# A decode step with paged attention: score and value products of four cached pages ranked ahead as one group

## The chip, the cores and the metric

The kernel runs on one core of a Trainium2 chip. The metric is the device time of one execution in microseconds (us); it is given as the median of three runs. Everything below that is read from a profile comes from one profiled execution on that core.

## What is computed

One inference step of a hybrid decoder layer, for a prompt of 512 tokens and a sample of 8 sequences with 4 new tokens each:

```python
z = rms_norm(x, g_mix) @ w_in              # columns: RWKV-7 | FoX | Conformer conv
ya = rwkv7_mix(za, ...); yb = fox_fn(q, k, v, logf); yc = conv_module(zc, ...)
x = x + concatenate([ya, yb, yc]) @ w_out
x = x + cross_attend(x, mk, mv, ...)       # 4 heads, 256 memory tokens
x = x + conv_ffn(x, ...)
```

The change touches one part of it, the sample's FoX attention over its cached keys and values (8 heads of 64 channels, 2048 cached tokens in 16 pages of 128 for each sequence; `kp` and `vp` are the pages that a table names):

```python
s_past = einsum('bqhd,bkhd->bhqk', q, kp) * scale + cT[..., :, None] + exT[..., None, :]
p = softmax(concatenate([s_past, s_new], axis=-1), axis=-1)
o = einsum('bhqk,bkhd->bqhd', p[..., :P], vp) + einsum('bhqk,bkhd->bqhd', p[..., P:], v)
```

All is float32. The large products with weights split both sides into a high and a low float32r part and add three products.

## The kernel before

One long function, `hybrid_step`, writes instructions through helpers (all matmuls stand on L186, all transposes on TensorE on L216). A scheduler then orders them: among the instructions that are ready for an engine it takes the one with the best rank, and the rank is the place in which the code wrote it, unless `tc.high_priority(n)` moves it ahead by n places. What comes out is a fixed order for each engine; each engine then goes through its own list, waiting where data or a buffer isn't there.

The stages follow each other: input norm and the first projection; RWKV, FoX and conv columns; the mixer's attention with the output projection; cross attention; feed-forward. The stage of this case is the mixer's attention. Two streams are woven in it (`weave`): `sample_past()`, the sample's attention over its cached pages, and `rest()`, which holds the end of the recurrence, the prompt's attention (`attend`, banks bank_r), the norm, keys and values of the memory (`memory`, products into bank_g from tiles xT, which first hold its operand), and the output projection `out_prompt` (products into bank_g from tiles four). The weave alternates their steps by estimated costs.

`sample_past` goes through the 8 batches. In round b it weaves `past_scores(b)` and `past_values(b - 2)`, with `past_weights(b - 1)` between. A step of either handles four of a batch's 16 pages, so that there are 32 steps of each:

- `past_scores`: POOL gathers four pages of keys into one of two buffers w_raw (`four_pages`, L1389: an indirect DMA, 128 partitions of 2048 numbers). DVE transposes them by blocks of 32 into one of two buffers KT (L1404). Then 16 products add into bank_s: four parts x of the channels by four strips of 32 rows (`QUAD`). Their stationary operand is 32 columns of Qx, which lies in a tile named w_hi. Behind the fourth step one product more (bank_s<-NX) adds the decay, the softmax's chain follows (L1299, L1415 to L1426), and bank_s is free for the next batch.
- `past_weights`: four transposes into bank_k and 16 small copies (L1439) make the weights PT, in a tile named w_lo.
- `past_values`: POOL gathers four pages of values into one of three buffers page (L1389). Then 4 products, one for each strip of 32 rows, add into bank_v; at the batch's end come four products with the step's own values (bank_v<-vs).

```python
            for x in range(4):
                for hp, po in enumerate(QUAD):
                    mm(acc[po, pg * 128: (pg + 1) * 128], Qx[:, 4 * hp + x]..., KT[:, :, 4 * hp + x], ...)
            yield 2.9
```

`sample_past` runs within `urgent(..., 0)`, which moves its instructions ahead by 0 places: they rank by where the weave puts them. In `out_prompt` POOL also adds squares (tot, L1670), each behind ACT (L1669).

Of the kernel before, what the change touches and what calls it, by code (L numbers as in the profile page):

```python
# [8 lines left out]
F32 = mybir.dt.float32  # L9
# [34 lines left out]
def _consts():  # L44
    """What depends on shapes alone: identities, masks, selections."""
# [46 lines left out]
    # rows (head, page of four, query) against pages, queries and columns of the like  # L92
# [18 lines left out]
def _past_consts():  # L111
    """of rows (head, page of four, query): causal mask, selections of pages, queries and columns"""
# [14 lines left out]
def _cross_consts():  # L127
    """of rows (head of two, 64 of the keys, token) those of a head and the 64; then selections of 32 rows, four times over"""
    p, m = np.arange(128)[:, None], np.arange(8)[None, :]
    own = [(m // 4 == h) & (m % 4 == p // 32) for h in range(2)]  # L130
    four = [p == 32 * x + np.arange(128)[None, :] % 32 for x in range(4)]
    return np.concatenate(own + four, 1).astype(np.float32)
# [5 lines left out]
def _pack_vectors(x):  # L138
    """Per-channel vectors side by side, a column for each 128 channels."""
# [15 lines left out]
def hybrid_step(tc, A):  # L155
# [62 lines left out]
    def rsqrt_from(out, in_, scale, eps):  # L218
        """out = (in * scale + eps) ** -0.5 by the logarithm and the exponential"""
        act(out=out, in_=in_, func=AF.Ln, scale=scale, bias=eps)  # L220
        act(out=out, in_=out, func=AF.Exp, scale=-0.5)

    def half_xyy(t, y, x, scale, eps):
        """t = (x * scale + eps) / 2 * y ** 2 for y, about the inverse root: (1.5 - t) * y is that root to the last bits"""
# [3 lines left out]
    def rsqrt_rows(out, x, n, scale, eps, eps_ap, work):  # L228
        """out = (x * scale + eps) ** -0.5 for n numbers to a partition"""
# [6 lines left out]
    def neg_sigmoid(t, e):  # L236
        """-1 / (1 + exp(-t)) in place, for t >= -40; by a Newton step"""
# [6 lines left out]
    def split(h, l, src, tt=vtt):  # L244
        """src = h + l exactly, both float32r"""
        acopy(h, src)
        tt(out=l, in0=src, in1=h.bitcast(F32), op=SUB)  # L247

# [18 lines left out]
    def weights(src, kb, cols, width=128, raws=None):  # L267
        """loads blocks of columns, two at most, and returns how to split each"""
# [37 lines left out]
    def gemm_steps(src, cols, xh, xl, evac, bank, spans=EVEN, kb=8, ahead=0, raws=None, first=None):  # L306
        """evac(ps, i, a) for span a of the i-th block of 128 columns; yields what each step costs TensorE"""
# [22 lines left out]
    def woven(*streams, first=False):  # L330
        """several streams side by side, each (its steps, their cost in all, where it sets in), in proportion; to the end of
        all or of the first"""
# [17 lines left out]
    def urgent(steps, ahead):  # L350
        """the steps, each before that many instructions of the others"""
# [27 lines left out]
    # what outlives the phases  # L379
# [16 lines left out]
    def four_blocks(n, dtype=F32R):  # L396
        """the places of four blocks of an operand, high or low"""
        return (yfp, yrp, xkp, xvp)[n].tile([128, 4, NT], dtype, name="four")

    yF = four_blocks(0, F32)  # first holds FoX's queries  # L400
# [5 lines left out]
    cum = cpl.tile([128, SEQ], F32R, name="cum")  # high parts from 0 and 64, low ones from 32 and 96  # L406
# [10 lines left out]
    # ================= inputs, first norm =================  # L417
# [20 lines left out]
    def norm_tok(xt, n, gain, ss, h, l, lo, work, bank, junk):  # L438
        """rows of xt, normed, transposed and split into columns lo.. of h and l"""
# [11 lines left out]
    # the operand is not yet divided by its root mean square: that follows after the products  # L451
# [4 lines left out]
    def roots(lo, n):  # L456
        """1 / root mean square of tokens lo .. lo + n, on all partitions"""
# [43 lines left out]
    # ================= gates of the cached keys =================  # L501
    # one row for each (batch, page), then (batch, head) by key, cumulated from the end
# [28 lines left out]
    # ================= RWKV columns, shifted by a token as they come =================  # L531
# [48 lines left out]
    # ================= RWKV: gates, keys, as their columns come =================  # L580
# [4 lines left out]
    def rmm(lhsT, rhs, evac):  # L585
        """float32 product with all 544 tokens of rhs, by halves"""
# [17 lines left out]
    def gates():  # L604
        """yields how many blocks of columns the next step needs"""
        yield 2
        # tanh(t) = 2 / (1 + exp(-2 t)) - 1
# [6 lines left out]
        # t1: minus the sigmoid of w, t4: that of a  # L614
# [6 lines left out]
        # decays: cumulated in each chunk, centred on half of the chunk's total  # L621
# [7 lines left out]
        # the step to the next chunk's centre, where that chunk's state will lie: [other half, block, head]  # L629
# [11 lines left out]
        # unit keys  # L641
# [40 lines left out]
    # where the cached keys and values lie: of four pages each, partition (page, k) takes rows 4 k .. 4 k + 3  # L682
# [13 lines left out]
    # ================= FoX and conv columns =================  # L696
# [9 lines left out]
    def finish(n=1):  # L706
        """what was put off until n more evacuations"""
# [5 lines left out]
    def evac_fl(ps, i, a):  # L713
        """forget gate: log_sigmoid(y) = -(max(-y, 0) + ln(1 + exp(-|y|)))"""
# [35 lines left out]
    def tok_major(dst, dst_s, src, src_s):  # L750
        """[128 channels, tokens] -> the prompt's token rows and the sample's"""
# [88 lines left out]
    def conv_taps():  # L840
        """the prompt's convolution: some taps on VectorE, the others by ScalarE and GpSimd"""
# [18 lines left out]
    def conv_ahead():  # L860
# [22 lines left out]
        for m in range(2):  # L883
            # the sample's windows, all taps at once: [batch * token, tap], by half the batches
# [11 lines left out]
    def rwkv_recurrence():  # L896
        def group_norm(y, n, heads, ps, work):
            """ps [n, heads, 64] -> y, each row of 64 centred and scaled"""
# [17 lines left out]
        # ================= RWKV: inverses of the blocks of 16 on the diagonals =================  # L916
        # N of (head, block of 128 tokens) as [chunk of two, block of 16, row] by column; with DVE's transposes by blocks
        # of 32 each of the 128 triangles comes to a partition (chunk, half, block of two, head and block of tokens)
# [48 lines left out]
        # ================= RWKV: sample, rows (head, batch, token) =================  # L967
        def sample_steps(rk, rk2):
# [43 lines left out]
            # -alpha S0 and rho S0, each row with its own batch  # L1012
# [37 lines left out]
            # the state after the four tokens  # L1050
# [18 lines left out]
        # ================= RWKV: chunks of 64, two to a block of 128 tokens =================  # L1069
# [4 lines left out]
        def chain(i, j, out):  # L1074
            """what a block and two heads need that no state enters, step by step"""
# [23 lines left out]
            # inverse of I - N by doubling blocks, from those of 16  # L1099
# [43 lines left out]
        def four(t, i):  # L1143
            """a block's columns as [head of two, its block, 64]"""
            return t[:, :, i * 128: (i + 1) * 128].rearrange("p j (r t) -> p j r t", r=2)

        def stateless(i):
            """of a block, in the places of what entered: AT (beta), RP (kap), the outputs (ynT) and the state (values) but for
            what the state before adds"""
# [36 lines left out]
        def stateful(i):  # L1186
            """the state, chunk after chunk: that of chunk ch lies in half ch % 2"""
# [51 lines left out]
    # what of the recurrence is left then runs beside the sample's attention  # L1239
# [38 lines left out]
    def recurrence_end():  # L1278
        """RWKV's group: ((norm * g + b) + bonus) * gate"""
# [9 lines left out]
        # where the residual will lie, the memory's operand  # L1289
# [3 lines left out]
        # causal mask, after nothing for the keys before  # L1293
# [7 lines left out]
    # ================= FoX: the prompt's attention, two heads at a time =================  # L1301
# [895 lines left out]
```

## Time and profile before

| | |
|---|---|
| median of three runs | 1304.64 us (1300.55 to 1308.29) |
| span of the profiled execution, first to last instruction | 1301.6 us; its own time isn't listed apart |
| TensorE (PE) busy | 1234.1 us, 95% |
| VectorE (DVE) busy | 809.1 us, 62% |
| ScalarE (ACT) busy | 501.2 us, 39% |
| GpSimd (POOL) busy | 290.6 us, 22% |
| moved by DMA | 173.83 MB, mean 134 GB/s |
| of it by POOL's queue, the gathers among it | 84.80 MB |

PE counts matmuls, PEld the loading of stationary operands, which runs beside them. Matmuls are pipelined, so that the records of matmuls that follow each other overlap: what a matmul adds is read from the chain of waits, where each piece begins at the end of the one before. "issue" is time in which an engine waited for nothing that the profile shows. A float32 product leaves two records in the trace.

### The profile page before, as it was taken

Reading aid. Unit: us, or ns where it says so; the run is one execution under the profiler, and the core shown is the slowest. Engines: PE = TensorE matmul, PEld = TensorE weight load, DVE = VectorE, ACT = ScalarE, POOL = GpSimd, SP = SyncE. Lnnn points to the kernel's source line nnn. Section 1 sums busy time; section 2 is a strip of 40 time slices with the busy share of each in tenths; the row PEclk is TensorE's granted clock in tenths of the full one; section 3 lists DMA queues with packets and bytes.
Section 4 is the critical chain, followed back from the end, with each engine's and each line's share of the span. In section 5 each row is a group of like instructions: output and inputs, shape, how many; then the busy total and the mean of one; then the engine's idle time right before and its main releaser. Section 6 shows DMA issues by size and latency. Waiting matters only on the chain.

```text
span 1301.6 us, 24852 instructions
## 1 busy us (share of the span) xinstructions
PE 1234.1 (95%) x10410; PEld 1011.6 (78%) x10410; DVE 809.1 (62%) x1514; ACT 501.2 (39%) x996; POOL 290.6 (22%) x322
## 2 busy tenths in 40 slices
PE   7899899999899999999998988999999999999997
PEld 6788788875555467654447875799999999999996
DVE  4699998765777377453234677557767424777631
ACT  5454543341456435221242422335444323444321
POOL 1262430033342131112223242012111100111120
PEclk9999999997699999999998998999999999999999
DMA  7221220221788497576663465033322323222231
GB/s 227 59 65 51 50 75 19 67 87 44 268 304 304 155 306 244 198 231 226 218 215 118 151 232 174 23 103 98 98 93 60 93 73 127 68 96 88 76 111 48
DMA packets 129649, 173.83 MB, mean 134 GB/s; under 512 B 7029, under 2 KB 110981, under 8 KB 121336
## 3 DMA queue, kind: packets, MB, share of 16 engines
q0 software_dynamic: 15216, 84.80, 18.1%
q1 hardware_dynamic: 88160, 70.76, 17.9%
q10 hardware_dynamic: 26160, 16.66, 4.4%
q8 instruction: 82, 1.34, 0.4%
q14 instruction: 31, 0.25, 0.1%
HBM read 164.54 MB, written 7.88 MB: 132 GB/s over the span
## 4 chain that ended last, share of the span: by engine, by line
PE 77%; DVE 9%; issue 5%; ACT 4%; DMA 3%; POOL 2%; SPq 0%; POOLq 0%; ACTq 0%; DVEq 0%
PE bank_g L186 42%; PE bank_r L186 10%; PE bank_d L186 6%; PE bank_s L186 6%; PE bank_v L186 4%; PE bank_a L186 2%; PE bank_r L216 2%; DVE w_lo L247 1%; PE bank_t L216 1%; PE bank_x L216 1%; DMA w_raw<-in_w_in_dram 1%; DMA w_raw<-in_w_out_dram 1%; DVE four L855 1%; DVE KT L1404 1%; ACT w_hi L177 1%
## 5 line engine op out<-in xcount | busy, mean ns | idle before, releaser
L186 PE MATMUL bank_g<-four,w_hi 128*128 128x272 f32 (+1 forms) x1536 | 284.7, 301 | 2.7 <-ACT w_hi L177 2.0
L177 ACT CAST w_hi<-w_raw 128x1024 fp32r<-128x1024 f32 (+3 forms) x149 | 140.6, 946 | 269.8 <-PE bank_g L186 206.1
L186 PEld LDWEIGHTS bank_g<-four,w_hi 128*128 128x128 f32 x1536 | 222.1, 189 | 26.4 <-issue 19.9
L247 DVE TENSOR_TENSOR w_lo<-w_raw,w_hi 128x1024 fp32r<-128x1024 f32 (+3 forms) x149 | 164.0, 1103 | 87.2 <-ACT w_hi L177 78.2
L186 PE MATMUL bank_g<-four,w_lo 128*128 128x272 f32 (+1 forms) x768 | 173.4, 301 | 0.5 <-DVE w_lo L247 0.5
L186 PEld LDWEIGHTS bank_g<-four,w_lo 128*128 128x128 f32 x768 | 122.1, 189 | 11.3 <-issue 8.6
L186 PE MATMUL bank_g<-act_h,w_hi 128*128 128x272 f32 (+2 forms) x400 | 124.6, 312 | 6.2 <-ACT w_hi L177 2.8
L186 PE MATMUL bank_g<-act_h,w_lo 128*128 128x272 f32 (+2 forms) x400 | 122.9, 308 | 0.0
L186 PE MATMUL bank_g<-act_l,w_hi 128*128 128x272 f32 (+2 forms) x400 | 122.0, 305 | 0.0
L2108 POOL TENSOR_SCALAR ysm<-HS,vec 128x32 f32<-128x32 f32 x44 | 42.0, 954 | 255.1 <-ACT HS L177 255.1
L1404 DVE STREAM_TRANSPOSE KT<-w_raw 128x2048 f32<-128x2048 f32 x32 | 73.5, 2302 | 23.9 <-PE bank_s L186 22.8
L186 PEld LDWEIGHTS bank_g<-act_h,w_hi 128*128 128x128 f32 x400 | 79.5, 199 | 10.5 <-ACT w_hi L177 3.2
L186 PEld LDWEIGHTS bank_g<-act_h,w_lo 128*128 128x128 f32 x400 | 79.1, 198 | 2.8 <-issue 1.2
L186 PEld LDWEIGHTS bank_g<-act_l,w_hi 128*128 128x128 f32 x400 | 79.4, 198 | 2.3 <-issue 1.1
L186 PE MATMUL bank_s<-KT,w_hi 128*32 128x128 f32 x1024 | 76.6, 292 | 3.4 <-DVE rsq L226 1.7
L186 PE MATMUL bank_d<-four,w_hi 128*128 128x272 f32 x384 | 78.1, 299 | 0.0
L186 PE MATMUL bank_g<-in_h,w_hi 128*128 128x272 f32 x352 | 73.6, 290 | 0.0
L186 PE MATMUL bank_g<-in_l,w_hi 128*128 128x272 f32 x352 | 73.5, 290 | 0.0
L186 PE MATMUL bank_g<-in_h,w_lo 128*128 128x272 f32 x352 | 73.2, 289 | 0.0
L186 PE MATMUL bank_v<-page,w_lo 128*32 128x512 f32 x256 | 67.8, 603 | 1.8 <-DMA page<-in_cache_fox_v_dram,kidx 1.8
L186 PEld LDWEIGHTS bank_s<-KT,w_hi 128*32 128x32 f32 x1024 | 39.2, 115 | 32.5 <-issue 19.8
L186 PEld LDWEIGHTS bank_d<-four,w_hi 128*128 128x128 f32 x384 | 61.9, 193 | 1.0
(631 smaller groups left out, 2458.6 us busy)
## 6 DMA issues: line engine op xcount, KB each, us to landing
w_raw<-in_w_up_dram SPq DMA_DIRECT2D x20, 1024.0 KB, 5.1
w_raw<-in_w_down_dram SPq DMA_DIRECT2D x16, 704.0 KB, 4.7
w_raw<-in_w_in_dram SPq DMA_DIRECT2D x17, 512.0 KB, 4.2
w_raw<-in_cache_mem_k_dram SPq DMA_DIRECT2D x16, 512.0 KB, 5.0
sV<-in_cache_mem_v_dram POOLq DMA_DIRECT2D x12, 512.0 KB, 6.4
w_raw<-in_w_in_dram SPq DMA_DIRECT2D x4, 1024.0 KB, 6.6
w_raw<-in_w_xk_dram ACTq DMA_DIRECT2D x8, 512.0 KB, 10.6
w_raw<-in_w_xv_dram ACTq DMA_DIRECT2D x8, 512.0 KB, 10.7
```

The lines of the kernel that those rows point to most:

```text
L177: nc.scalar.copy(out, in_)
L186: pinned(nc.tensor.matmul(out, lhsT, rhs, start=start, stop=stop, skip_group_check=True))
L216: pinned(nc.tensor.transpose(out=out, in_=in_, identity=ident[p0:p0 + k, p0:p0 + k]))
L247: tt(out=l, in0=src, in1=h.bitcast(F32), op=SUB)
L855: vstt(out=yp, in0=U[:, m, w: w + SEQ], scalar=w_tap, in1=yp, op0=MUL, op1=ADD)
L1404: nc.vector.transpose(out=KT, in_=K)
L2108: nc.gpsimd.tensor_scalar(out=ysm, in0=H[:, 2:6, 1:], scalar1=w[2], scalar2=b, op0=MUL, op1=ADD)
```

## The change

The 16 score products of a step, and the 4 value products of a step, are put into a block of rank 600 places ahead. Nothing else that runs is changed; the remaining lines of the diff take out comments and docstrings, so that line numbers behind move by one or two.

```diff
@@ past_scores
             KT = KT.rearrange("p (j c k) -> p j c k", j=4, k=32)
-            for x in range(4):
-                for hp, po in enumerate(QUAD):
-                    mm(acc[po, pg * 128: (pg + 1) * 128], Qx[:, 4 * hp + x].rearrange("p m q -> p (m q)"), KT[:, :, 4 * hp + x], pg == 0 and x == 0, False)
+            with tc.high_priority(600):
+                for x in range(4):
+                    for hp, po in enumerate(QUAD):
+                        mm(acc[po, pg * 128: (pg + 1) * 128], Qx[:, 4 * hp + x].rearrange("p m q -> p (m q)"), KT[:, :, 4 * hp + x], pg == 0 and x == 0, False)
             yield 2.9
@@ past_values
             t = four_pages(page(), "cache_fox_v", b, pg)
-            for j, po in enumerate(QUAD):
-                mm(acc[po], PT[:, j, pg * 32: pg * 32 + 32], t[:, j * 512: j * 512 + 512], pg == 0, False)
+            with tc.high_priority(600):
+                for j, po in enumerate(QUAD):
+                    mm(acc[po], PT[:, j, pg * 32: pg * 32 + 32], t[:, j * 512: j * 512 + 512], pg == 0, False)
             yield 2.9
```

What the scheduler makes of it. On PE, in the output projection, before: a value product (bank_v) stands between products of bank_g.

```order
L216 MATMUL bank_k<-ident,w_hi 128x128 x4
L186 MATMUL bank_g<-four,w_hi 128x512
L186 MATMUL bank_v<-page,w_lo 32x512
L186 MATMUL bank_g<-four,w_lo 128x512
L186 MATMUL bank_v<-page,w_lo 32x512
L186 MATMUL bank_g<-four,w_hi 128x512
L186 MATMUL bank_v<-page,w_lo 32x512
L186 MATMUL bank_g<-four,w_hi 128x512
L186 MATMUL bank_v<-page,w_lo 32x512 x5
```

Three products of one step stand alone and the fourth with the four of the next step. On PE with the change, in the same projection:

```order
L186 MATMUL bank_g<-four,w_hi 128x512
L186 MATMUL bank_v<-page,w_lo 32x512 x12
L216 MATMUL bank_k<-ident,w_lo 128x128 x2
L186 MATMUL bank_g<-four,w_hi 128x512
L216 MATMUL bank_k<-ident,w_lo 128x128
```

Three steps of value products follow each other without a product of bank_g between. Also on PE with the change, in the memory's products (bank_g from xT):

```order
L186 MATMUL bank_g<-xT_3987,w_lo 128x256
L186 MATMUL bank_v<-page,w_lo 32x512 x3
L186 MATMUL bank_s<-KT,w_hi 32x128 x3
L186 MATMUL bank_v<-page,w_lo 32x512 x9
L186 MATMUL bank_s<-KT,w_hi 32x128 x13
L186 MATMUL bank_g<-xT_3987,w_hi 128x256
```

A step of scores and three steps of values stand in one block, between which no product of another bank is left. On POOL, at the end of the stage, before: the gathers (DMA page and DMA w_raw) and the adds to tot.

```order
L1389 DMA page<-in_cache_fox_v_dram,kidx 128x2048
L1670 TENSOR_TENSOR tot<-tot,res_sq 128x512
L1389 DMA page<-in_cache_fox_v_dram,kidx 128x2048
L1389 DMA w_raw<-in_cache_fox_k_dram,kidx 128x2048
L1389 DMA page<-in_cache_fox_v_dram,kidx 128x2048
L1670 TENSOR_TENSOR tot<-tot,res_sq 128x512
L1389 DMA w_raw<-in_cache_fox_k_dram,kidx 128x2048
L1389 DMA page<-in_cache_fox_v_dram,kidx 128x2048
L1670 TENSOR_TENSOR tot<-tot,res_sq 128x512
L1389 DMA page<-in_cache_fox_v_dram,kidx 128x2048 x2
```

And with the change:

```order
L1389 DMA w_raw<-in_cache_fox_k_dram,kidx 128x2048
L1389 DMA page<-in_cache_fox_v_dram,kidx 128x2048 x3
L1672 TENSOR_TENSOR tot<-tot,res_sq 128x512
L1389 DMA page<-in_cache_fox_v_dram,kidx 128x2048
L1672 TENSOR_TENSOR tot<-tot,res_sq 128x512 x2
L1389 DMA page<-in_cache_fox_v_dram,kidx 128x2048 x2
```

The last gathers of keys now stand ahead of the first add, and fewer gathers of values stand behind one.

## Rows read from the trace of the kernel before

**Rows 1.** The page: span, and PE's busy time, share and instructions
```profile
span 1301.6 us, 24852 instructions
...
PE 1234.1 (95%) x10410; PEld 1011.6 (78%) x10410; DVE 809.1 (62%) x1514; ACT 501.2 (39%) x996; POOL 290.6 (22%) x322
```

**Rows 2.** Busy time by stage: stretch, its length, each engine (count), clock, DMA share, GB/s
```profile
core 0: us, PE busy (x) PEld busy (x) DVE busy (x) ACT busy (x) POOL busy (x), PEclk, DMA share, GB/s
0.00:330.00 330.00, 302.56 (x2888) 257.96 (x2888) 254.55 (x539) 140.32 (x274) 96.83 (x116) 0.95 0.27 78
330.00:700.00 370.00, 351.88 (x2630) 202.70 (x2629) 202.75 (x386) 145.09 (x352) 91.60 (x86) 0.96 0.67 234
700.00:1301.60 601.60, 579.64 (x4896) 550.94 (x4895) 351.81 (x591) 215.79 (x371) 102.19 (x122) 0.99 0.32 102
```

**Rows 3.** The page's groups: count, busy us, mean ns of one, idle before
```profile
L1404 DVE STREAM_TRANSPOSE KT<-w_raw 128x2048 f32<-128x2048 f32 x32 | 73.5, 2302 | 23.9 <-PE bank_s L186 22.8
...
L186 PE MATMUL bank_s<-KT,w_hi 128*32 128x128 f32 x1024 | 76.6, 292 | 3.4 <-DVE rsq L226 1.7
...
L186 PE MATMUL bank_v<-page,w_lo 128*32 128x512 f32 x256 | 67.8, 603 | 1.8 <-DMA page<-in_cache_fox_v_dram,kidx 1.8
```

**Rows 4.** Chain of waits, 540 to 700 us: start, length, what, records merged
```profile
542.54 0.55 PE bank_s L186 x10
...
572.23 0.34 PE bank_s L186 x2
572.57 0.43 PE bank_g L186
...
582.86 0.97 PE bank_v L186 x2
...
614.98 1.00 PE bank_v L186 x8
...
645.59 1.01 PE bank_s L186 x32
...
672.22 3.00 PE bank_g L186 x12
```

**Rows 5.** Chain of waits, 497 to 524 us, in the memory's products
```profile
497.71 5.34 PE bank_g L186 x45
...
504.04 0.36 PE bank_s L186 x8
...
508.93 0.34 PE bank_s L186 x2
509.26 0.31 PE bank_g L186
```

**Rows 6.** Waits, 330 to 700 us: who waited for whom, us, times, longest
```profile
POOL page L1389 <- PE bank_v L186: 101.1, 17, 16.9
...
POOL w_raw L1389 <- DVE KT L1404: 50.6, 11, 15.6
POOL tot L1670 <- ACT res_sq L1669: 43.8, 6, 16.5
```

**Rows 7.** DMA, 330 to 700 us: sum; gathers by count, us from issue to landing
```profile
DMA packets 39285, 86.46 MB, mean 234 GB/s; under 512 B 1599, under 2 KB 30286, under 8 KB 31320
...
page<-in_cache_fox_v_dram,kidx POOLq DMA_INDIRECT x32, 7.8
...
w_raw<-in_cache_fox_k_dram,kidx POOLq DMA_INDIRECT x30, 7.0
```

**Rows 8.** Three answers, columns as in rows 2; the first has POOL's gathers (L1389) alone
```profile
357.80:404.50 46.70, 14.32 (x14) 1.00 0.82 307
...
357.80:404.50 46.70, 44.20 (x453) 25.21 (x452) 36.50 (x73) 28.87 (x84) 16.47 (x16) 1.00 0.82 307
...
490.00:510.00 20.00, 20.00 (x189) 17.08 (x187) 16.77 (x42) 12.67 (x27) 3.31 (x3) 1.00 1.08 360
```

**Rows 9.** Timeline at the stage's end: start, length, instruction [idle before <- releaser]
```profile
660.80 1.49 POOL L1389 DMA_INDIRECT page<-in_cache_fox_v_dram,kidx  x1 [5.81 <-PE bank_v L186]
...
667.77 1.06 PE L186 MATMUL bank_v<-page,w_lo 128*32 128x512 f32 x8 [1.75 <-DMA page<-in_cache_fox_v_dram,kidx]
```

## The prediction

> **What bounds the kernel now.** I read the page first. TensorE (PE) is busy 1234.1 of a span of 1301.6 us [rows 1]; but a busy share is a mean over stages, so next come windows by stage. The change touches only the stage from about 330 to 700 us, where the cached pages are attended: 370 us, PE busy 351.9, DVE 202.8, ACT 145.1, POOL 91.6, DMA share 0.67 [rows 2]. So here too PE is the bound; its idle time is 370 - 351.9 = 18.1 us. The reader should then ask what PE's busy time is made of, and the chain of waits, which lists PE's work piece by piece, answers that.
>
> The trace counts two records for each float32 product: 1024 of bank_s are 512 score products (32 groups of 16), 256 of bank_v are 128 value products (32 groups of 4) [rows 3]. Each writes a strip of 32 of the 128 rows of a bank; the four products of four strips can run beside each other, if they follow each other. The pieces show the price of not doing so [rows 4]. Four value products in a row (x8) take 1.00 us; one of them alone between two products of bank_g takes 0.97. Sixteen score products in a row (x32) take 1.01; one alone takes 0.34. And the product of bank_g behind such a break takes 0.43, against 3.00 / 12 = 0.25 in a row of twelve; in the memory's products it is 0.31 against 5.34 / 45 = 0.12 [rows 5]. Alternating costs both sides.
>
> **The change, part by part.** No instruction is added, removed or given another operand; only ranks change. So the terms are counts of runs, taken from the two orders of the built programs, times prices from rows.
>
> *Value products.* Before, the 128 products stand in 62 runs: 40 single, 19 of two to four, 2 of five, 1 of ten. At 0.97 for a single, 1.00 for two to four, 0.25 a product in longer runs: 38.8 + 19 + 2.5 + 2.5 = 62.8 us. After, 34 runs: 10 single, 19 of two to four, 1 of five, 2 of nine, 2 of twelve: 9.7 + 19 + 1.25 + 4.5 + 6 = 40.5. Gain 22.3 us.
>
> *Score products.* Before, 138 runs: 99 of one or two at 0.34, 15 of three to five at 0.36 to 0.55 [rows 4, 5] (0.45), 7 of seven to thirteen at some 0.7 (0.06 a product and a drain), 16 of sixteen or seventeen at 1.01, one of 27 at 1.7: 33.7 + 6.8 + 4.9 + 16.2 + 1.7 = 63.3 us. After, 37 runs: 3 single, 8 of three to thirteen at about 0.6, 24 of sixteen, 2 of 32: 1.0 + 4.8 + 24.2 + 4.0 = 34.0. Gain 29.3 us.
>
> *The other side of each break.* Before, 118 stretches of score or value products are followed by a product of bank_g; after, 16. 102 x 0.18 to 0.19 = 19 us. The products of the prompt's attention (bank_r) are broken less often too; I count that at nothing, since the waits that it runs into are not priced.
>
> All of this lies on PE, which the stage waits for, so the gross gain is 22.3 + 29.3 + 19 = 70.6 us.
>
> The Trainium skill ("TensorE: Matmul & The Clock Gate", Measured speedup vs the span model) speaks for less: three column tiles of 512 columns gave 2.38 there, not 3. By that a group of four would take 0.97 x 3 / 2.38 = 1.22 us (an estimate), 32 groups 7 us more than I count. The row's 1.00 us, 3.9 times better than four single ones, decides here.
>
> *What is late next.* The ranked groups come earlier among the other work of PE, and PE takes its instructions in the program's order: a group whose page has not landed now holds up all that stands behind it. The unshown cost is these waits. Pages come by gathers that POOL issues, 1.05 MB each by shape; issue to landing is 7.8 us for values, 7.0 for keys [rows 7], and keys are then transposed on DVE in 2.3 us [rows 3]. Before, POOL waited 101.1 us for value products to free a page and 50.6 for transposes to free a key buffer [rows 6]: transfers waited for PE, so they have slack. Cover that goes: the memory's products, between which groups now stand packed. From the 21st score group to the 28th, the new order has 8 score and 8 value groups and 174 products of the memory: 8.1 + 8 + 174 x 0.12 = 37 us, with some 5 of other products 42. Its transfers are 16 gathers and 174 / 24 = 7 weight blocks of 0.52 MB, 20.5 MB. The best 20 us of this stage moved 360 GB/s, a stretch with 14 gathers in 46.7 us moved 307 [rows 8]: 57 to 67 us. Three page buffers, two key buffers, two transposed ones and five weight slots can hold up to 9.9 MB ahead, which leaves 30 to 35 us. So the wait there is 0 to 25 us. I take 10, nearer the lower end, because that stretch of 14 gathers ran with PE busy 44.2 of 46.7 us: even pages at that pace cost 0.2 us each. Behind it the order has 177 memory products and 40 transposes without a group, in which the transfers catch up.
>
> By the Trainium skill's limit of about 358 GB/s from HBM for a core ("DMA: Bandwidth & Descriptors", Specifications) the stretch needs 57 us, as by my faster row; the trace shows it reached for 20 us only, so the slower row stays in the bounds.
>
> At the stage's end eight value pages share three buffers. Before, a gather issued at 660.80 was used at 667.77, with 1.75 us of PE idle [rows 9]; after, five groups follow so closely that 0 to 2 us each may be waited: 0 to 10, I take 5. Against that, eleven gathers stood on POOL behind the first of its adds to tot, which waited 43.8 us for ACT [rows 6]; now it is six. I count nothing for it. The 18.1 us of idle time stay.
>
> Sum: 70.6 - 10 - 5 = 55.6 us. The profiled execution has a span of 1301.6; the median of the three runs, 1304.64, is 3.0 above, which I put down to what lies around the span and to scatter (1300.55 to 1308.29). 1304.6 - 55.6 = **1249 us**. A measurement of this kernel tells about 0.5% (6.5 us) from no change.
>
> **Rivals.**
> 1. *Groups wait at the head of PE's queue* (slower). Place: the 17 score groups from the 12th to the 28th and the 27 value groups from the 6th on, 44 groups that the new order puts right behind the release of a buffer. If each waits 3 us alone, of 7.8 for a value page or 7.0 + 2.3 for keys, that is 132 us against 70.6: 1304.6 + 61 = 1366 us. It decides from 70.6 / 44 = 1.6 us a group. For it: leads in the order are short. Against it: 14 gathers in 46.7 us with 2.5 us of idle PE [rows 8], 0.2 us each, in a stretch whose leads were just as short. Chance 0.07. That PE never lets a ready matmul pass a waiting one is also what the Trainium skill says ("TensorE: Matmul & The Clock Gate", Part 3, The mechanism); no row here shows it by itself.
> 2. *Transfers become the bound of the middle* (faster, by half). If the buffers are not full when the packed stretch begins, the wait is 25 us and not 10, the tail's is 10, and a late batch carries over to the next: 35 us in all, 1304.6 - 36 = 1269 us. For it: the 307 GB/s. Against: 360 GB/s were reached while weights and pages came together. Chance 0.25.
> 3. *Nothing waits more.* Gross gain, 4 us more from bank_r and half of the idle 18: 1304.6 - 84 = 1221 us. For it: POOL's 101.1 us of waiting. Against: it needs full buffers throughout. Chance 0.12.
> 4. *The change doesn't group, or the gain is covered.* The order shows runs of 16 and 4, so only a transfer that ends the stage could hide it: 86.5 MB at 307 GB/s are 282 us, under the 370 [rows 2, 7]. 1304 us, chance 0.03.
>
> **How the numbers follow.** The forecast (1236 to 1262: waits of 2 to 28 us) has 0.53. With it the range takes in case 2 up to its upper bound (gain 20: 1285) and case 3: 1220 to 1285, leaving out cases 1 and 4 (0.10) and the ends of the others. Faster is forecast, cases 2 and 3: 0.90. Within 0.5% is case 4: 0.03. Slower is case 1: 0.07.
>
> **What would show it.** The stage shrinks from 370 to about 315 us. In the chain, bank_s appears as x32 of 1.01 us and bank_v as x8 of 1.00; PE bank_v x2 of 0.97 is rare; bank_g in a row is at 0.25 and 0.12. PE's idle time in the stage grows from 18 to some 33 us, with DMA of pages and DVE KT as its releasers, and the DMA rate from 234 to about 275 GB/s. Wrong: PE waits for pages or KT above 70 us in sum; runs in which strips still take 0.97 each; a stage that ends later than PE's work because of something else.

## The result, and the profile after

The change makes the kernel faster: 1252.72 us median (1249.94 to 1254.88, four runs) against 1303.14 us (1300.55 to 1308.29, four runs of before on the same chip). The ratio is 0.961, with a 95% interval of 0.9585 to 0.9635. The gain is 50.4 us where 55.6 were forecast.

The profiled execution took 1253.36 us. Its page, span and engines (before: [rows 1]):

```profile
span 1251.6 us, 24835 instructions
...
PE 1162.3 (93%) x10410; PEld 998.9 (80%) x10410; DVE 810.1 (65%) x1516; ACT 499.6 (40%) x994; POOL 290.0 (23%) x322
```

The busy time by stage, with the columns of [rows 2]; the stage of the change now ends near 650 us and not near 700:

```profile
0.00:330.00 330.00, 300.64 (x2881) 255.53 (x2881) 253.08 (x532) 139.73 (x271) 95.19 (x114) 0.95 0.26 75
330.00:650.00 320.00, 282.89 (x2645) 193.46 (x2645) 206.22 (x396) 144.26 (x352) 93.77 (x89) 0.94 0.78 274
650.00:1251.60 601.60, 578.73 (x4889) 549.97 (x4887) 350.83 (x589) 215.64 (x371) 101.03 (x121) 0.99 0.32 102
```

The stages ahead and behind are as they were: PE is busy 300.6 us ahead (302.6 before) and 578.7 us behind (579.6), in nearly as many matmuls. All of the difference lies in the middle one: 370 us became 320. PE's busy time there fell from 351.9 to 282.9, 69.0 us less; its idle time rose from 18.1 to 320 - 282.9 = 37.1, 19.0 us more. 69 - 19 = 50.

The chain of waits from 330 to 650 us (start, length, what, records merged) shows the groups:

```profile
368.87 0.97 PE bank_v L186 x2
...
436.25 0.86 PE bank_v L186 x8
...
490.02 1.45 PE bank_v L186 x8
...
512.84 1.01 PE bank_s L186 x32
...
617.82 1.00 PE bank_v L186 x8
```

Sixteen score products in 1.01 us and four value products in 1.00 are now the usual piece; a single value product (x2 of 0.97) has become rare. To see what each kind costs PE, I added up in the trace, for each matmul, how far its end lies behind the end of the matmul before it (330 to 700 us, no idle time counted). All later readings of "what a kind adds" are this sum:

| adds on PE, us | before | after | saved |
|---|---|---|---|
| score products (bank_s from KT) | 63.4 | 37.0 | 26.4 |
| value products (bank_v from page) | 61.4 | 39.7 | 21.7 |
| memory (bank_g from xT) | 57.4 | 50.5 | 6.9 |
| projection (bank_g from four) | 59.8 | 50.0 | 9.8 |

Together 64.8 of the 69.0 us. The waits in the stage, who for whom (us, times, longest), show where the new idle time lies (before: [rows 6]):

```profile
POOL w_raw L1389 <- DVE KT L1404: 62.6, 13, 20.0
POOL page L1389 <- PE bank_v L186: 39.9, 7, 24.9
POOL tot L1672 <- ACT res_sq L1671: 39.1, 7, 9.3
...
ACT w_hi L177 <- DMA w_raw<-in_w_out_dram: 10.7, 2, 6.9
...
PE bank_v L186 <- DMA page<-in_cache_fox_v_dram,kidx: 8.8, 4, 4.0
...
PE bank_g L186 <- ACT w_hi L177: 6.2, 3, 5.0
```

and the timeline has the places of the longest (start, length, instruction, idle before it and its releaser):

```profile
490.02 1.45 PE L186 MATMUL bank_v<-page,w_lo 128*32 128x512 f32 x8 [2.57 <-DMA page<-in_cache_fox_v_dram,kidx]
...
507.86 1.06 PE L186 MATMUL bank_v<-page,w_lo 128*32 128x512 f32 x8 [1.44 <-DMA page<-in_cache_fox_v_dram,kidx]
...
550.93 0.80 PE L186 MATMUL bank_g<-four,w_hi 128*128 128x512 f32 x1 [5.05 <-ACT w_hi L177]
551.66 3.64 PE L186 MATMUL bank_s<-KT,w_hi 128*32 128x128 f32 x64
...
578.88 1.56 PE L186 MATMUL bank_v<-page,w_lo 128*32 128x512 f32 x8 [3.98 <-DMA page<-in_cache_fox_v_dram,kidx]
```

Value groups at the head of PE's queue wait for their pages, 8.8 us in sum where it was 1.8 [rows 3]. The 5.05 us are a product of the projection whose weights came late: ACT, which makes w_hi of them, waited 10.7 us for the transfer.

A long wait seems to cost more than its idle time. About the end of each of these three longest (2.57, 5.05 and 3.98 us) the granted clock, 1.00 until then, fell to 0.50 for some us, which is 1.2 GHz in place of 2.4 (the third number from the right):

```profile
490.60:494.00 3.40, 3.40 (x20) 2.60 (x13) 0.57 (x2) 0.49 (x1) 0.00 (x0) 0.50 1.03 412
548.70:555.30 6.60, 4.37 (x66) 3.27 (x67) 3.47 (x3) 1.63 (x2) 0.00 (x0) 0.50 1.02 355
579.40:582.60 3.20, 3.20 (x13) 1.84 (x6) 1.39 (x2) 0.63 (x1) 0.00 (x0) 0.50 1.04 411
```

There two groups of scores took 3.64 us (551.66), where a group takes 1.01 otherwise, and a group of values 1.45 and 1.56 us and not 1.06 as behind the shorter wait at 507.86. Not every fall goes with a wait: the clock stood at 0.50 from 456 to 460 us too, and in the 60 us ahead PE had not waited for as much as 1 us at a time.

POOL waits for PE much less than before (39.9 us, 101.1 in [rows 6]): the transfers' slack was used up, as the DMA's sums show (before: [rows 7]):

```profile
DMA packets 39646, 87.68 MB, mean 274 GB/s; under 512 B 1648, under 2 KB 30352, under 8 KB 31681
...
w_raw<-in_w_out_dram ACTq DMA_DIRECT2D x8, 512.0 KB, 15.2
...
page<-in_cache_fox_v_dram,kidx POOLq DMA_INDIRECT x32, 8.7
...
w_raw<-in_cache_fox_k_dram,kidx POOLq DMA_INDIRECT x30, 7.9
```

The projection's weights, which now take 15.2 us from issue to landing, took 6.5 before:

```profile
w_raw<-in_w_out_dram ACTq DMA_DIRECT2D x8, 512.0 KB, 6.5
```

### The profile page after: what moved, and what is told of

It reads as the page before. It is cut to its first block, busy times and chain, and to the rows that moved or that the text cites. A ratio compares the mean times of both kernels' runs of the same rounds, so it can differ in the third digit from the quotient of the medians.

```text
span 1251.6 us, 24835 instructions
## 1 busy us (share of the span) xinstructions
PE 1162.3 (93%) x10410; PEld 998.9 (80%) x10410; DVE 810.1 (65%) x1516; ACT 499.6 (40%) x994; POOL 290.0 (23%) x322
## 4 chain that ended last, share of the span: by engine, by line
PE 65%; DVE 12%; issue 9%; DMA 6%; ACT 5%; POOL 2%; SPq 0%; POOLq 0%; ACTq 0%; DVEq 0%
PE bank_g L186 39%; PE bank_r L186 8%; PE bank_d L186 7%; PE bank_s L186 3%; DMA page<-in_cache_fox_v_dram,kidx 3%; PE bank_a L186 2%; PE bank_v L186 2%; DMA w_raw<-in_cache_fox_k_dram,kidx 2%; DVE KT L1404 2%; DVE w_lo L247 2%; PE bank_r L216 1%; PE bank_t L216 1%; DMA x_tok<-in_x_prompt_dram 1%; PE bank_x L216 1%; ACT w_lo L1440 1%
## 5 line engine op out<-in xcount | busy, mean ns | idle before, releaser
L186 PE MATMUL bank_g<-four,w_hi 128*128 128x272 f32 (+1 forms) x1536 | 277.5, 299 | 5.7 <-ACT w_hi L177 5.0
L186 PEld LDWEIGHTS bank_g<-four,w_hi 128*128 128x128 f32 x1536 | 221.9, 188 | 15.2 <-ACT w_hi L177 5.3
L1404 DVE STREAM_TRANSPOSE KT<-w_raw 128x2048 f32<-128x2048 f32 x32 | 73.5, 2301 | 11.7 <-DMA w_raw<-in_cache_fox_k_dram,kidx 10.7
L2102 DVE TENSOR_TENSOR up<-bank_g,tot 128x544 f32<-128x544 f32 x44 | 31.8, 722 | 44.6 <-PE bank_g L186 44.6
L1389 POOL DMA_INDIRECT w_raw<-in_cache_fox_k_dram,kidx x32 | 36.0, 1125 | 94.2 <-DVE KT L1404 62.6
L186 PE MATMUL bank_d<-four,w_lo 128*128 128x272 f32 x192 | 56.7, 295 | 0.0
## 6 DMA issues: line engine op xcount, KB each, us to landing
w_raw<-in_w_xk_dram ACTq DMA_DIRECT2D x8, 512.0 KB, 12.4
```

What stands on the lines that cost most here:

```text
L186: pinned(nc.tensor.matmul(out, lhsT, rhs, start=start, stop=stop, skip_group_check=True))
L1389: nc.gpsimd.indirect_dma_start(out=t, out_offset=None, in_=A[cache][0].rearrange("n (k j) h d -> (n k) (j h d)", j=4), in_offset=bass.Indi ...
L1404: nc.vector.transpose(out=KT, in_=K)
L2102: vtt(out=two(x[:, 2:]), in0=ev2(ps), in1=two(rstd), op=MUL)
```

## The experiments

My theory: the gain is the count of broken runs on PE, less what PE then waits for transfers. Its rivals: that being early is what gains, whatever the grouping; that the strips running side by side play no part, only the breaks do; and, for the new idle time, that it isn't the transfers. Each kernel's ratio is to runs of before on the same chip.

### Each group alone

One of the two ranks is set to 0.

```diff
@@ past_values (scores alone ranked)
-            with tc.high_priority(600):
+            with tc.high_priority(0):
@@ past_scores (values alone ranked, the other kernel)
-            with tc.high_priority(600):
+            with tc.high_priority(0):
```

> Only the score products keep the rank of 600 places ahead; the value products go back to their own rank. In the order the score products stand in 30 runs (138 before, 37 with the change), the value products in 59 (62, 34), and 36 stretches (118, 16) are followed by a product of bank_g. Theory (what counts is how many runs and breaks stand on TensorE): 29 us from scores, 2 from values, 82 x 0.185 = 15 from breaks, less some 8 of new waits: about 38 us under the kernel before, 1265 us. Rival (what counts is how far ahead the groups stand in the order; here the last batches' scores stand about where they stood before): 0 to 15 us, 1288 to 1303 us.

> Only the value products keep the rank of 600 places ahead. In the order the value products stand in 27 runs, the score products in 144, and 99 stretches are followed by a product of bank_g. Theory (runs and breaks): 22 us from values, -1 from scores, 19 x 0.185 = 3.5 from breaks, less some 5 of new waits: about 20 us under the kernel before, 1283 us; with the kernel of scores alone the two gains add to that of the whole change. Rival (value pages freed earlier let POOL gather earlier, and that is the gain): most of the 50 us here already, 1255 to 1265 us.

Scores alone: 1270.48 us, ratio 0.9712 (0.9658 to 0.9765), 35.5 us gained. Values alone: 1293.79 us, 0.989 (0.9842 to 0.9937), 12.2 us. The sum, 47.7, is the change's 50.4 within the scatter: the two parts add. Scores brought what was expected, values less. With values alone ranked, the value products add 37.8 us on PE, 23.6 less than before; but the scores, still in 144 runs, rose to 66.9, bank_r from 69.8 to 72.9 and PE's idle time from 18.1 to 27.1; and memory and projection cost 117.2 us as before, since the order still has 99 of 118 breaks. The saving on the other side of the breaks belongs to the scores: with them alone ranked, memory and projection add 100.7 us (100.5 with the change).

### The order inside a group

The sixteen score products keep their rank and their place; only the two loops change places, so that four products into the same strip follow each other.

```diff
-                for x in range(4):
-                    for hp, po in enumerate(QUAD):
+                for hp, po in enumerate(QUAD):
+                    for x in range(4):
```

> The change with the two loops of the score products exchanged: the four products of a strip follow each other, and strip after strip. Runs and breaks are those of the change (38, 35, 16). Theory (the strips of a run lie beside each other on TensorE): the 16 products of a group come one after the other at about 0.34 - 0.13 = 0.21 us, 3.5 us a group instead of 1.01; 32 x 2.5 = 80 us more work, of which some 15 to 20 fall into the waits that the change has: about 1315 us, slower than the kernel before. Rival (what a lone product costs is the break in the array's use alone, not the strip): the time of the change, 1253 us.

1279.03 us, 0.9785 (0.9739 to 0.9831): half of the gain is lost. Its chain of waits:

```profile
360.97 2.39 PE bank_s L186 x32
```

A group takes 2.39 us where neighbouring strips gave 1.01. The score products add 76.2 us (32 x 2.39 = 76.5), 39 more than with the change, while idle time fell from 41.0 to 23.0 us (330 to 700 us): transfers and transposes get time again, and some 25 us are left of the 39. So the order of the strips counts, and it is not the whole of the grouping: sixteen lone products at 0.34 [rows 4] would be 5.4 us, sixteen in a row into one strip after another 2.39, sixteen with the strips taking turns 1.01. That strips overlap is seen in the value products, of which four in a row take 1.00 us and one 0.97 [rows 4]. But four score products in a row into one strip also add to the same numbers of the bank one after the other; how much of the 2.39 us comes from that, no run separates. I had expected 1315 us from a group of some 3.5 us, and that price was wrong; that 15 to 20 us of it would fall into waits came true (18.0).

### How far ahead

```diff
-            with tc.high_priority(600):
+            with tc.high_priority(100):
```

(in both places, and with 64 in the second kernel)

> The change with a rank of 100 places ahead instead of 600. In the order, 43 and 37 runs, 11 breaks towards bank_g: grouped almost as with 600, but from the sixth batch on the groups stand less far ahead (the 25th score group stands some 12 us of TensorE's work later than with 600, the 17th value group 40). Theory (runs and breaks): the work on TensorE as with 600, and fewer waits for pages: 1243 to 1255 us. Rival (lead): a third to a half of the gain, 1275 to 1285 us.

> The change with a rank of 64 places in place of 600. The built order has 73 runs of scores, 49 of values and 47 breaks: between before (138, 62, 118) and the change (37, 34, 16). Theory (the gain is the count of runs and breaks times what each costs): of what each saved in the change, 65/101 of 26 us for scores, 13/28 of 22 us for values, 71/102 of 17 us for the other side, 39 us on TensorE, less some 8 of the 19 us of new idle: about 1272 us (1265 to 1280). Rival (being ahead by any number of places is what gains): as the change, 1248 to 1256.

With 100: 1251.74 us, 0.9603 (0.9549 to 0.9656), the same as with 600. With 64: 1287.92 us, 0.9866 (0.9802 to 0.993), a third of the gain. What decides is thus not how early, but whether the rank is enough to keep a group whole. My 1272 for the second was wrong in its arithmetic: I had scaled the saving with the number of runs, but the order of rank 64 still has 28 single value products, and its chain of waits is full of this:

```profile
534.34 0.31 PE bank_g L186
534.65 0.98 PE bank_v L186 x2
```

A single product costs as much as a whole group, so the saving goes by products that are alone, not by runs. The value products add 58.7 us, 2.7 less than before, where I had 10; the scores add 49.7 (13.7 less, of 17 expected), memory and projection 103.2 (14.0 less, of 12), and idle time rose by 12.4, not 8. The prompt's bank_r, which I had left out, adds 5.2 us more than before.

### The whole chain ahead

The kernel before, with no group ranked, but with all of `sample_past` moved 600 places ahead; and the change with 300 places in addition.

```diff
-    weave((urgent(sample_past(), 0), 135.0), (rest(), 148.0, 0.06))
+    weave((urgent(sample_past(), 600), 135.0), (rest(), 148.0, 0.06))
```

> The kernel before with all of the sample's attention ranked 600 places ahead, without a group of its own for the products. In the order 40 and 38 runs, 11 breaks. Theory (runs and breaks count, whatever brings them about): about the gain of the change, 1240 to 1255 us. Rival (the group of its own is what counts): less than half of it, above 1280 us.

> The change, and all else that the sample's attention writes ranked 300 places ahead as well (gathers, transposes, softmax, copies). In the order 35 and 34 runs, 7 breaks towards bank_g; the last value group stands some 50 us of TensorE's work earlier than with the change, ahead of the output projection. Theory (the change's remaining 37 us of idle TensorE come from pages and transposes that are late, and from the tail of a batch's scores that ranks low, while transfers pause): the work on TensorE as in the change, idle time some 25 us instead of 37: 1240 us. Rival (transfers are the bound in the packed part, so that packing it further only moves the waits): 1250 to 1265 us.

1275.38 us, 0.9761 (0.9723 to 0.9799), for the first; 1271.63 us, 0.9753 (0.9708 to 0.9797), for the second. Both missed my numbers, and both are slower than the change. The first has whole groups too (40 runs of scores, 38 of values; they add 39.5 and 38.7 us) and its sums on PE are near the change's. But PE's idle time from 330 to 700 us is 55.3 us against the change's 41.0, and the first rows of PE's own waits say why:

```profile
PE bank_k L216 <- ACT w_hi L1425: 14.9, 4, 12.2
PE bank_s L186 <- DVE KT L1404: 10.0, 8, 3.4
```

The transposes of the softmax weights (bank_k) now stand at the head of PE's queue and wait for ACT to scale them, once for 12.2 us. The 14.3 us of idle time are the larger part of the 23 us by which this kernel is slower than the change; the mean granted clock of the profiled execution is lower too (0.952 against 0.965), and how the rest divides is open. Moving a whole chain ahead moves also its instructions that depend on slow steps; moving the matmuls alone does not. The second kernel's four runs scatter from 1256.76 to 1276.21 us and its profile is of the 1256.76, so what costs its median 19 us is left open; the other three show a mean granted clock of 0.950 to 0.956, this one 0.961.

### More groups, earlier gathers

The change with the transposes of `past_weights` and the four last products of a batch (bank_v from vs) and their transposes ranked as groups too; and the change with gathers and DVE's transposes ranked with their products.

```diff
@@ past_weights (more groups)
+        with tc.high_priority(600):
+            for pg in range(4):
+                tr(ps[:, pg * 128: (pg + 1) * 128], S[:, pg * 128: (pg + 1) * 128])
@@ past_values (earlier gathers, the other kernel)
+            with tc.high_priority(600):
+                t = four_pages(page(), "cache_fox_v", b, pg)
```

> The change, and the four transposes of past_weights, the four products with the step's own values and the four transposes of the rows behind them each as a group ranked 600 ahead. These are 8 x 12 products, of which in the change about half stand alone at 0.22 to 0.3 us and break the others. Theory: up to 8 x (4 x 0.25 - 0.45) = 4 us for each of the three kinds at most, some 5 us in all after waits: 1247 us; the value runs rise to 43 in the order, which takes 2 us back. Rival: these products wait for ACT's and DVE's copies, and ranked ahead they hold up TensorE: 1255 to 1265 us.

> The change, and the gathers and the transposes of keys on DVE ranked 600 places ahead too; softmax and copies keep their rank. In the order 29 and 35 runs, 15 breaks. Theory (late pages): the waits for pages and KT, some 20 of the 37 us, fall by half: 1243 us. Rival (what frees the buffers sets the gathers' time, not their rank, so that they can't go earlier): 1250 to 1256 us.

More groups: 1251.52 us, 0.9584 (0.9549 to 0.9619), the same as the change: the value products' sum rose by 7.1 us and the idle time fell by 6.2. Earlier gathers: 1273.08 us, 0.9757 (0.9719 to 0.9796), 20 us slower than the change. Idle time is not the reason (39.0 us from 330 to 700 us against 41.0). Its windows, with the granted clock as the third number from the right:

```profile
370.00:410.00 40.00, 36.73 (x193) 16.69 (x191) 24.21 (x64) 19.14 (x51) 10.15 (x10) 0.79 0.67 256
410.00:450.00 40.00, 36.17 (x395) 20.12 (x396) 28.64 (x57) 19.29 (x58) 10.54 (x12) 0.91 0.59 212
450.00:490.00 40.00, 33.30 (x318) 24.73 (x313) 25.97 (x45) 13.59 (x31) 12.54 (x11) 0.91 0.92 329
```

and the same of the change:

```profile
370.00:410.00 40.00, 35.94 (x385) 19.90 (x383) 32.22 (x62) 23.50 (x66) 13.09 (x12) 1.00 0.83 302
410.00:450.00 40.00, 36.95 (x427) 22.35 (x428) 27.74 (x72) 26.44 (x82) 15.30 (x15) 1.00 0.81 308
450.00:490.00 40.00, 32.71 (x326) 25.92 (x324) 29.18 (x43) 16.99 (x33) 13.22 (x11) 0.96 1.05 362
```

From 370 to 490 us PE is about as busy in both, but does fewer matmuls (193, 395 and 318 records against 385, 427 and 326), at a granted clock of 0.79 to 0.91 against 0.96 to 1.00. The 0.79 is a mean of two levels. Parts of the first window, and a group of values within the second part:

```profile
370.00:382.00 12.00, 9.52 (x74) 5.03 (x72) 7.73 (x22) 5.85 (x16) 3.30 (x4) 1.00 0.76 289
382.00:399.00 17.00, 16.21 (x51) 6.32 (x51) 11.48 (x31) 10.50 (x25) 3.89 (x4) 0.50 0.73 279
...
383.46 1.93 PE L186 MATMUL bank_v<-page,w_lo 128*32 128x512 f32 x8
```

Ahead of the fall PE was busy 9.52 of 12 us and waited twice, for 1.04 and 1.44 us; then a group of values took 1.93 us, where it takes 1.00 at the full clock. A lower clock shows as busy time, not as waiting. In the three windows from 370 us, 40 us times what the clock lacks to 1 gives 8.4 + 3.6 + 3.6 = 15.6 us against 1.6 with the change. By kinds, bank_r adds 76.8 us from 330 to 700 us (7.5 more than with the change) and the value products 46.6 (6.9 more). How much of the 20 us the clock makes, and why it falls there and not with the change, no run settles.

### Without the transfers

The value products all read one page that is gathered once, so that 31 of the 32 value gathers are left out; in the change, and in the kernel before. In a third kernel one page of keys stands for all keys and all values of the change.

```diff
+            if not kept_page:
+                kept_page.append(four_pages(page(), "cache_fox_v", b, pg))
+            t = kept_page[0]
-            t = four_pages(page(), "cache_fox_v", b, pg)
```

> The change, but only the first of the 32 gathers of value pages is made and all 128 value products read that one page: 31 gathers of 1.05 MB are left out. The built order on TensorE has 36 runs of scores, 33 of values and 12 breaks, as the change has 37, 34 and 16. Theory (the 37 us that TensorE still idles in the stage are mostly late transfers, of values directly and of keys and weights by sharing the queues): idle falls to about 20 us, the waits for pages (10 us) are gone, and the time is about 1235 us (1228 to 1242). Rival (transfers are early enough, the idle is the order's own): at most the 10 us of page waits move to another place and the time stays at 1247 to 1253.

> The kernel before, with the same 31 gathers of value pages left out. Runs 141 of scores, 70 of values, 128 breaks, as before has 138, 62 and 118. Theory (before, transfers hide behind a TensorE that is broken up; PE alone sets the stage's end): the time stays within 6 us of before, 1297 to 1310, and TensorE's idle in the stage stays at 15 to 20 us. Rival (transfers set part of the time before too): 1285 or less, idle under 8 us.

> The change, but one page of keys is gathered and stands for all 32 steps' keys (each step still transposes it) and all steps' values: 63 of the 64 gathers are left out, some 66 MB. TensorE's order has 40 runs of scores, 35 of values (20 of them single, where the change has 10, which by their prices adds 7 us) and 10 breaks. Theory (what TensorE idles in the stage of the change above the 18 us of before is late gathers, of keys as much as of values): idle from 330 to 700 us falls from 41 to 18 to 24 us, and the time is about 1240 us (1234 to 1245). Rival (the idle is mostly the order's own: groups that wait for the transposes of their keys, for the softmax's chain and for the projection's operands): idle stays above 28 us, the time is 1247 to 1258.

The change without value gathers: 1248.26 us, 0.9578 (0.952 to 0.9636). Without any but one: 1249.48 us, 0.9572 (0.9532 to 0.9612). Both stand where the rival put them, 3 to 5 us under the change, and within the scatter. The stage without value gathers and without gathers, in the columns of [rows 2], and PE's waits in the second:

```profile
330.00:650.00 320.00, 292.40 (x2646) 197.32 (x2646) 205.96 (x386) 143.17 (x352) 56.92 (x55) 0.93 0.52 173
330.00:650.00 320.00, 286.47 (x2647) 195.47 (x2648) 209.86 (x406) 144.52 (x356) 27.35 (x29) 0.94 0.23 71
```

```profile
PE bank_s L186 <- DVE KT L1407: 6.2, 6, 2.4
PE bank_k L186 <- POOL page L1376: 3.2, 1, 3.2
PE bank_s L186 <- DVE rsq L226: 2.9, 1, 2.9
PE bank_g L186 <- ACT sq L1544: 2.6, 2, 1.3
PE bank_s L186 <- POOL w_hi L1400: 2.5, 3, 1.3
```

Without gathers the DMA rate is 71 GB/s, not 274; no wait for a page is left, nor the 5.05 us for the projection's weights; and still PE idles 33.5 us of the 320 (37.1 with the change). The change's waits for transfers (8.8 us for pages and up to 6.2 behind w_hi) were real, but beneath them lay others: score groups wait for DVE's transposes of their keys (6.2 us, 3.7 with the change) and for the softmax's and the recurrence's small steps. Part of the missing gain is the order: without gathers the scheduler leaves more value products alone (20, not 10), and they add 43.8 us, not 39.7. Without the value gathers alone this hides more: PE idles 27.6 us of the 320, 9.5 less than with the change and about as much as the page waits were, but the value products add 51.6 us, 11.9 more, and the time hardly falls. So these two times alone don't give the transfers' price.

The kernel before without value gathers is slower than before: 1317.38 us, 1.0111 (1.0046 to 1.0175). Neither theory had that. Idle time fell (18.1 to 12.5 us), though not under the 8 that the rival asked, but the value products now stand in 70 runs, 55 of them single, and add 73.6 us instead of 61.4. The prices of the prediction, applied to this order (55 singles, 9 runs of two to four, 3 of five, one each of seven, nine and thirteen), give 53.4 + 9 + 3.75 + 7.25 = 73.4. The chain shows them:

```profile
600.44 0.97 PE bank_v L186 x2
601.42 0.43 PE bank_g L186
601.84 0.97 PE bank_v L186 x2
602.82 0.43 PE bank_g L186
```

A kernel that moves 32 MB less and is 16 us slower, because fewer products of four stand together, is the clearest support that the theory of the runs has.

## Why the prediction was right

*The bound.* PE's busy time set the stage, and the stage shrank by what PE saved less what it waited. Shown by the stage's two rows; and with gathers left out PE's idle time in the stage fell by 3.6 to 9.5 us and the time by 3 to 5, so that transfers are a part of the waits and not the bound.

*Value products.* 22.3 us forecast, 21.7 measured. The price of a run held for the change (40.5 forecast, 39.7 measured) and for an order it wasn't made from (73.4 and 73.6). The Trainium skill ("TensorE: Matmul & The Clock Gate", Measured speedup vs the span model) has a speedup of 2.38 for three column tiles, by which 32 groups would have cost 7 us more than I counted (an estimate); the sum of 39.7 us does not have them. The trace's 1.00 us decided rightly.

*Score products.* 29.3 us forecast, 26.4 measured: the groups cost 37.0 and not 34.0, and I had priced every group at 1.01 us. That is their price at the full clock. The first four ran at the lower one for the most part:

```profile
348.66 1.94 PE L186 MATMUL bank_s<-KT,w_hi 128*32 128x128 f32 x32 [2.62 <-DVE rsq L226]
```

They add 7.1 us together, and the two behind the wait for the projection's weights 3.6: 4.6 us more than six at 1.01; the rest came a little cheaper than counted.

*The other side of each break.* 19 us forecast, 16.7 measured (6.9 and 9.8).

*bank_r.* Counted at nothing, and nearly that: by the same sum 69.8 us before and 69.3 with the change. The rest of PE's saving, 69.0 - 64.8 = 4.2 us, lies mostly in transposes (bank_k) and in the lone products beside the groups (bank_s from NX, bank_v from vs), which the table leaves out.

*Gross.* 70.6 us forecast, 69.0 measured. So close a sum is partly luck: the three terms were 5.8 us too large together, and 4.2 us came from what wasn't counted.

*New waits.* 15 us forecast, 19.0 measured. For pages the places were right: 490 to 508 us, in the packed stretch of the memory's products (2.57 and 1.44 us, where I had 10), and towards the stage's end (3.98 at 578.9 us and 0.82 at 608.9, where I had 5). They come to 8.8 us and not 15; before it was 1.8. What I had not named is the late weights of the projection (5.05 us at one place, their transfers from issue to landing 15.2 us); scores wait 3.7 us for their keys. So the sum came near by other waits than those it was made of, which is luck too. And the notion behind the term, that these waits are the transfers' price, holds in part only: without the value gathers 9.5 us of idle time went, without any but one gather 3.6, and other waits stood in their place. The eleven gathers that I counted behind POOL's first add to tot are twelve in the trace; the sum does not use them.

*The numbers of the forecast.* The stage came out at 320 us (315 forecast), PE's idle time at 37 (33), the DMA rate at 274 GB/s (275).

*The rivals.* Groups at the head of the queue (1366 us): a wait of 1.6 us for each of 44 groups was needed, and in sum PE waited 8.8 us for pages and 3.7 for transposes. Transfers as the bound (1269 us): the DMA rate stood at 362 GB/s over 40 us (450 to 490) and at 386 over the best 20, so the slower end of my bounds, 307 GB/s, was no limit, and without the gathers the time hardly falls.

```profile
476.00:496.00 20.00, 16.48 (x141) 12.04 (x140) 14.26 (x26) 7.85 (x13) 6.19 (x5) 0.91 1.05 386
```

The Trainium skill gives about 358 GB/s as HBM's limit for a core ("DMA: Bandwidth & Descriptors", Specifications); the trace goes above it, and the measurement decides. Nothing waits more (1221 us): refuted by the 37 us of idle time. No change: refuted.

## What to carry to other kernels

Where products write a strip of 32 of a bank's 128 rows, keep those of all four strips together and let the strips take turns: a lone product cost as much as the whole group (0.97 against 1.00 us here), and each break cost the full-width neighbour 0.18 us more. Rank the matmuls alone, as far ahead as keeps the group whole (100 places did as well as 600 here, 64 did not); a whole chain moved ahead puts its slow steps at the head of the queue. Price such a change by the products that stay alone in the built order, and don't count a wait's removal as gain before the work behind it is seen to be ready.

## What was not expected of the hardware

- Sixteen products into strips in the order 1-1-1-1-2-2-2-2 took 2.39 us, in the order 1-2-3-4-1-2-3-4 1.01 us, the same instructions with the same operands; not 3.5 us, as I had put it.
- About the end of waits of 2.57 to 5.05 us the granted clock fell to 0.50 for 3 to 7 us, and a group of values took 1.45 and 1.56 us there, not 1.00.
- Beginning gathers and transposes earlier made the stage slower without more idle time: the granted clock was 0.79 in the mean from 370 to 410 us (0.50 from 382 to 399), where the change had 1.00.
- Without the value gathers the DMA rate fell by a third (173 GB/s in the stage, 274 with the change), but a gather of keys still took 6.7 us to land, against 7.9: at the lower rate it took 1.2 us less, and most of the time stayed.
